# A hybrid attention and gMLP backbone: attention and its beginning rewritten as lists of steps, with a merged softmax and values in two passes

## The chip, the core and the metric

The kernel runs on one core of a Trainium2 chip. The metric is the device time of one execution in microseconds; before the change the median of three runs is 1554.76 us (1552.0 to 1555.82).

## What is computed

Two layers over 512 latent tokens of 1024 channels (a grid of 8 rows by 64 columns) with 256 context tokens, all in float32. Layer 0 mixes tokens by neighbourhood attention, layer 1 by a gated MLP over positions; each is followed by a squared-ReLU MLP. Every sub-layer begins with an RMS norm and a shift and scale that come from a conditioning vector (adaLN). The change touches layer 0's norm, its QKV products, its attention and the first part of its output projection. Of the reference, cut:

```python
q, k, v = jnp.split(h @ w_qkv, 3, axis=-1)          # 16 heads of 64
q = rms_norm(heads(q), q_g)
k = rms_norm(heads(k), k_g)
kc, vc = jnp.split(hc @ w_qkv[:, D_MODEL:], 2, axis=-1)
kc = rms_norm(heads(kc), k_g)
...
s_lat = einsum('bjqhd,bkjmhd->bhjqkm', q_r, k_r) * scale + bias
s_ctx = einsum('bjqhd,blhd->bhjql', q_r, kc) * scale
s = concatenate([s_lat, s_ctx], axis=-1)
p = softmax(s, axis=-1)
o = einsum(p_lat, v_r) + einsum(p_ctx, vc)
...
x = x + g1 * (y @ w_o)
x = x + g2 * squared_relu_mlp(modulate(rms_norm(x, norm2_g[i]), sh2, sc2), mlp_w1[i], mlp_w2[i])
```

## The kernel before

Channels lie on the 128 partitions, in eight chunks k, and tokens on the free axis. Every float32 product is made of three float32r products: both operands are parted into a high part (a cast, on ScalarE) and a low part (value less cast, on VectorE), and high by high, high by low and low by high are added up in PSUM (`products`, L178). The weights lie in one array `wall`, cut into units of 128 x 1536 (`UNIT`); class `Weights` (L48) loads a unit from HBM on SP's queue into one of two buffers `raw`, casts it in four parts into `whi` and `wlo` (L80, L81; three buffers of each), and `get` casts units ahead of their use by `ahead`.

In the beginning (L214 to L367) the instructions of TensorE, VectorE and ScalarE are pinned to program order (`in_order`, `pe_`, `vec_`, `act_`). `squares` and `root` make the norm's sum: a square, three folding additions on VectorE, one matmul with `ones`, a square root, a reciprocal. `ada_load` and `ada_rows` compute shift and scale for a group g of two chunks: 64 small matmuls, a copy of the row, its transpose, four small additions. `chunks` scales two chunks of the input and parts them into `h_hi`, `h_lo` (latent) or `hc_hi`, `hc_lo` (context); `lat_products` and `con_products` add these chunks into the QKV tiles of head pair 0, which stay open in six PSUM areas `o0`. At the end 16 matmuls spread the conditioning vector over the partitions (`cb`, L357 to L362).

Then eight pairs of heads follow (L561 to L579). `a_tile(p, t)` makes QKV of pair p for 128 tokens: latent tiles t = 0 to 3 (24 matmuls of 384 columns), context tiles 4 and 5 (24 of 256 columns, k and v alone); it squares and copies the result and parts v into `vh` and `vl`. Two heads lie in these tiles with 64 columns of zeros between, so that a window of 128 columns holds one head and zeros. After some tiles comes `ada_block` (L378), one row of the adaLN products for later use: a DMA of 512 KB and a multiplication with a sum on VectorE. `a_final(p)` normalizes q and k (a square root on ScalarE, three multiplications on VectorE, two on GpSimd), transposes them in three groups (`split`, L455) and parts them into `th` and `tl` (two buffers), from which 16 DMAs on SP's queue fill `kk`, `q1` and `q2`. `scores(n)` makes the scores of head n in four blocks of 128 queries by 512 keys (256 of a neighbourhood, 256 of the context) and the softmax: a maximum over the context half, bias and maximum over the other, two exponentials with sums, a reciprocal, a scaling on GpSimd. `values(n)` goes through six key tiles; for each, `turn` transposes the two to four blocks of probabilities that see it and parts them into `ph` and `pl` (two buffers each), and three products with `vh` and `vl` add to one PSUM bank `o` for both heads of a pair. The output projection follows (`residual`, L605): the first four output tiles are multiplied k by k, the others one by one, the last three in two halves of the tokens with the next norm between.

In the pairs the order on each engine is not pinned: a planner sorts instructions by program order and by when it takes them to be ready. PSUM has eight banks: three `mm`, two `t` (transposes), two `s` (scores and sums), one `o`.

## Time and profile before

| | us |
|---|---|
| median of three runs (1552.0 to 1555.82) | 1554.76 |
| the profiled execution | 1551.22 |
| its span | 1549.4 |
| TensorE busy | 1506.5 |
| VectorE busy | 925.4 |
| ScalarE busy | 663.8 |
| GpSimd busy | 138.1 |

Times in the rows are counted from the start of the span. A matmul's end is modelled, so a busy TensorE is not yet one at its peak: the distance from one start to the next tells more than a duration. In a row of the timeline, x4 says that four instructions in a row are put together, and the brackets name idle time before them and what ended it. The rows that the prediction uses stand further below.

### The profile page before, as it was taken

The numbers are of one execution on the slowest core, as the hardware profiler recorded it, in microseconds if no ns is written. First come the engines' busy times: TensorE is split into PE (matmuls) and PEld (weight loads), VectorE is DVE, ScalarE is ACT, GpSimd is POOL, SyncE is SP. The second block draws the span as 40 slices with busy tenths as digits, with TensorE's granted clock in tenths as the row PEclk, the third lists the DMA queues.
The fourth block names the chain that finished last, engine by engine and source line by source line (L and its number), as shares of the span: only waits on it lengthen the run. The fifth ranks groups of instructions, "written<-read, shape, count | busy, mean of one in ns | idle before, by whom it ended". The sixth has DMA issues, their size and how long they took to land.

```text
span 1549.4 us, 21490 instructions
## 1 busy us (share of the span) xinstructions
PE 1506.5 (97%) x7960; PEld 1289.4 (83%) x7960; DVE 925.4 (60%) x1953; ACT 663.8 (43%) x1569; POOL 138.1 (9%) x162
## 2 busy tenths in 40 slices
PE   4999999999999999999999999999999999999999
PEld 3888888887898888888978887888889988888888
DVE  4778777777776555665565568644456743334431
ACT  3566666675544322442443366323234532234320
POOL 0122222222200000000100013100001000000000
PEclk9999999999999999999999999999999999999999
DMA  9365555535146555556233325323221333223330
GB/s 319 137 178 172 169 165 162 168 114 165 65 143 209 199 199 191 196 192 205 90 107 136 115 93 164 118 93 115 86 95 44 140 103 100 86 100 102 102 110 28
DMA packets 69224, 212.08 MB, mean 137 GB/s; under 512 B 8320, under 2 KB 27392, under 8 KB 68736
## 3 DMA queue, kind: packets, MB, share of 16 engines
q1 hardware_dynamic: 57600, 200.57, 39.4%
q10 hardware_dynamic: 11520, 10.15, 2.2%
q8 instruction: 62, 1.02, 0.3%
q14 instruction: 42, 0.34, 0.1%
HBM read 193.91 MB, written 2.10 MB: 127 GB/s over the span
## 4 chain that ended last, share of the span: by engine, by line
PE 69%; DVE 3%; issue 0%; ACT 0%; DMA 0%; ACTq 0%; DVEq 0%
PE ps_mm L183 34%; PE ps_t L183 23%; PE ps_o L183 11%; PE ps_s L755 1%; DVE wlo L81 1%; DVE nt L172 1%; DVE hl L174 0%; DVE xall L611 0%; DMA raw<-wall 0%; PE ps_s L156 0%; DVE acc L151 0%; DVE u L761 0%; ACT v L731 0%; DVE v L733 0%; DVE hl L170 0%
## 5 line engine op out<-in xcount | busy, mean ns | idle before, releaser
L80 ACT CAST whi<-raw 128x384 fp32r<-128x384 f32 x620 | 278.4, 511 | 352.4 <-PE ps_mm L183 150.2
L81 DVE TENSOR_TENSOR wlo<-raw,whi 128x384 fp32r<-128x384 f32 x620 | 329.2, 579 | 143.3 <-ACT whi L80 142.9
L380 DVE CUSTOM_DVE_ANT_0 adaraw<-adaraw,cb 128x1024 f32<-128x1024 f32 x80 | 99.2, 1240 | 98.3 <-DMA adaraw<-ada 98.2
L183 PE MATMUL ps_mm<-hh,wlo 128*128 128x512 f32 (+1 forms) x416 | 154.0, 370 | 0.6 <-DVE wlo L81 0.6
L183 PE MATMUL ps_mm<-hh,whi 128*128 128x512 f32 (+1 forms) x416 | 154.2, 371 | 0.0
L183 PE MATMUL ps_mm<-hl,whi 128*128 128x512 f32 (+1 forms) x416 | 153.8, 370 | 0.0
L183 PE MATMUL ps_mm<-ml,whi 128*128 128x512 f32 (+1 forms) x336 | 120.7, 359 | 0.0
L183 PE MATMUL ps_mm<-mh,wlo 128*128 128x512 f32 (+1 forms) x336 | 120.5, 359 | 0.0
L183 PE MATMUL ps_mm<-mh,whi 128*128 128x512 f32 (+1 forms) x336 | 120.5, 359 | 0.0
L183 PE MATMUL ps_mm<-wlo,hh 128*128 128x384 f32 (+1 forms) x320 | 113.2, 354 | 0.7 <-DVE wlo L81 0.7
L183 PE MATMUL ps_mm<-whi,hh 128*128 128x384 f32 (+1 forms) x320 | 113.2, 355 | 0.0
L183 PE MATMUL ps_mm<-whi,hl 128*128 128x384 f32 (+1 forms) x320 | 113.0, 354 | 0.0
L183 PE MATMUL ps_t<-hh,whi 128*128 128x512 f32 (+1 forms) x280 | 104.4, 373 | 0.0
L183 PE MATMUL ps_t<-hl,whi 128*128 128x512 f32 (+1 forms) x280 | 104.1, 372 | 0.0
L183 PE MATMUL ps_t<-hh,wlo 128*128 128x512 f32 (+1 forms) x280 | 103.9, 371 | 0.0
L183 PEld LDWEIGHTS ps_mm<-hh,wlo 128*128 128x128 f32 x416 | 78.5, 189 | 13.7 <-DVE wlo L81 0.8
L183 PEld LDWEIGHTS ps_mm<-hl,whi 128*128 128x128 f32 x416 | 78.5, 189 | 12.6
L183 PEld LDWEIGHTS ps_mm<-hh,whi 128*128 128x128 f32 x416 | 78.5, 189 | 12.6
L665 ACT CAST mh<-relu 128x512 fp32r<-128x512 f32 x64 | 39.7, 622 | 95.1 <-DVE relu L662 95.1
L611 DVE SCALAR_TENSOR_TENSOR xall<-ps_mm,mod,xall 128x512 f32<-128x512 f32 (+1 forms) x47 | 30.7, 657 | 68.7 <-PE ps_mm L183 68.7
L541 ACT CAST ph<-ps_t 128x512 fp32r<-128x512 f32 (+2 forms) x96 | 45.2, 481 | 61.9 <-PE ps_t L538 56.4
L183 PEld LDWEIGHTS ps_mm<-mh,whi 128*128 128x128 f32 x336 | 63.5, 189 | 9.4
(229 smaller groups left out, 3387.9 us busy)
## 6 DMA issues: line engine op xcount, KB each, us to landing
raw<-wall SPq DMA_DIRECT2D x155, 768.0 KB, 4.4
adaraw<-ada SPq DMA_DIRECT2D x80, 512.0 KB, 3.8
aw<-ada SPq DMA_DIRECT2D x32, 256.0 KB, 7.1
bt<-bias_t SPq DMA_DIRECT2D x16, 512.0 KB, 3.8
q<-th SPq DMA_DIRECT2D x32, 128.0 KB, 2.4
q<-tl SPq DMA_DIRECT2D x32, 128.0 KB, 2.4
bc<-lngb ACTq DMA_DIRECT2D x12, 256.0 KB, 3.5
x0l<-x0T SPq DMA_DIRECT2D x2, 1024.0 KB, 9.6
```

Source lines behind the costliest of these rows:

```text
L80: nc.scalar.copy(out=hi[:, cs], in_=raw[:, cs])
L81: nc.vector.tensor_tensor(out=lo[:, cs], in0=raw[:, cs], in1=hi[:, cs], op=ALU.subtract)
L172: vec.scalar_tensor_tensor(out=t, in0=xk, scalar=A[:, k:k + 1], in1=r, op0=ALU.mult, op1=ALU.mult)
L183: eng.matmul(o, lhsT=a, rhs=b, start=start and i == 0, stop=stop and i == n - 1, skip_group_check=shared)
L380: vec.tensor_tensor_reduce(out=a, in0=a, in1=cb, scale=1.0, scalar=0.0, op0=ALU.mult, op1=ALU.add, accum_out=mod[:, idx:idx + 1])
L541: act.copy(out=ph[:, cs], in_=tb[:, cs])
L611: vec.scalar_tensor_tensor(out=x[m][:, c0:c1], in0=o[:, c0:c1], scalar=gate(m), in1=x[m][:, c0:c1], op0=ALU.mult, op1=ALU.add)
L665: act.copy(out=a, in_=r)
L755: pe.matmul(s[:, n * P:(n + 1) * P], lhsT=v[:, n, g * P:(g + 1) * P], rhs=ws, start=True, stop=True)
```

## The change

It does four things.

- In the beginning, `squares` comes in two halves; `total` adds up chunks by several matmuls in place of the folding additions (all eight chunks for the first half of the tokens, four after one addition for the others); the conditioning vector is spread first; `ada_rows` is cut into the matmuls and `ada_cols`; weights are cast part by part between other work (`casts`), and `lat_products` takes one chunk k and some of the tiles t, so that products, adaLN matmuls, sums and transposes alternate.
- The pairs become lists of steps: `a_steps` (one k of one tile), `f_steps` (norm, context keys, keys, queries), `s_steps` (one block of scores), `v_steps` (one key tile). `weave` puts the QKV steps of the next pair, or at the end the first output tiles (`o_steps`), evenly between the steps of scores and values. The probabilities of a key tile are multiplied two steps after they were turned.
- Scores of both halves get bias (zeros for the context), sign and extremum in one instruction of 512 columns and one exponential; a reciprocal is made for two blocks at a time.
- `vh` and `vl` of one head lie side by side in 128 columns of `vv`, and each key tile is multiplied by `ph` and by `pl` only. A head ends with `finish`: one half of the partitions of its bank is copied and added to the other.

The 24 rows of adaLN that are computed in the pairs are spread otherwise (`ADA`). The diff, cut to its core; the lines that it takes out are left out here, as they stand in the kernel above, and so are bodies that only move, such as the DMAs of keys and queries:

```diff
+        def squares(i):
             sq = pre.tile([P, KC, TC], F32, tag="psq", bufs=2, name="psq")
+            for ks in (slice(0, KC // 2), slice(KC // 2, KC)):
+                act_.activation(out=sq[:, ks], in_=x0[i][:, ks], func=AF.Square)
             return sq
...
+        def fold(sq):
+            h = KC // 2
+            vec_.tensor_tensor(out=sq[:, :h], in0=sq[:, :h], in1=sq[:, h:], op=ALU.add)
+        def total(sq, n):
             sps = bank("s", 2)
+            for k in range(n):
+                pe_.matmul(sps[:, :TC], lhsT=ones, rhs=sq[:, k], start=k == 0, stop=k == n - 1)
+            return sps[:, :TC]
+        def root(total, rr):
+            act_.activation(out=rr, in_=total, func=AF.Sqrt, scale=1.0 / D, bias=eps)
+            vec_.reciprocal(out=rr, in_=rr)
...
+            return row
+        def ada_cols(g, row):
             tp = bank("t", 2)
...
+            for k, t in zip(ks, ts):
                 vec_.scalar_tensor_tensor(out=t, in0=xs[:, k], scalar=A[:, k:k + 1], in1=rr, op0=ALU.mult, op1=ALU.mult)
                 act_.activation(out=hi[k], in_=t, func=AF.Identity, bias=B[:, k:k + 1])
+            for k, t in zip(ks, ts):
                 vec_.scalar_tensor_tensor(out=lo[k], in0=t, scalar=B[:, k:k + 1], in1=hi[k], op0=ALU.add, op1=ALU.subtract)
...
+        def lat_products(k, ts=range(4)):
+            for t in ts:
+                qkv_products(o0[t], t, W.get("qkv", k), k, eng=pe_)
...
+        act_.activation(out=junk, in_=eps, func=AF.Sqrt)
...
         for n in range(2):
             o = bank("s", 2)
             for i in range(4):
+                pe_.matmul(o[:, i * P:(i + 1) * P], lhsT=cc[:, 4 * n + i, 0:1].broadcast_to([P, P]), rhs=ident,
+                           start=True, stop=True)
+            act_.copy(out=cb[:, n * 512:(n + 1) * 512], in_=o)
+        sa = squares(0)
+        ta = total(sa, KC)
+        sb = squares(1)
+        fold(sb)
+        tb = total(sb, KC // 2)
+        root(ta, rl[:, :TC])
+        root(tb, rl[:, TC:])
+        row = ada_rows(0, aw[0])
+        cast = W.casts(act_, vec_)
+        cast[0]()
+        ada_cols(0, row)
+        chunks(0, lat, (), cast[1:])
+        sc = squares(2)
+        fold(sc)
+        lat_products(0)
+        row = ada_rows(1, aw[1])
+        lat_products(1, range(2))
+        ada_cols(1, row)
+        lat_products(1, range(2, 4))
+        chunks(1, lat)
+        tc_ = total(sc, KC // 2)
+        root(tc_, rc)
+        cast = W.casts(act_, vec_)
+        for step in cast:
+            step()
+        lat_products(2)
+        chunks(0, con)
+        row = ada_rows(2, aw[2])
+        lat_products(3, range(2))
+        ada_cols(2, row)
+        lat_products(3, range(2, 4))
+        chunks(1, con)
+        con_products(0)
+        chunks(2, lat)
+        con_products(1)
+        lat_products(4)
+        row = ada_rows(3, aw[3])
+        chunks(2, con)
+        lat_products(5, range(2))
+        ada_cols(3, row)
+        lat_products(5, range(2, 4))
+        con_products(2)
+        chunks(3, lat)
+        lat_products(6)
+        for step in W.casts(act_, vec_):
+            step()
+        lat_products(7)
+        chunks(3, con)
+        con_products(3)
+        for step in W.casts(act_, vec_):
+            step()
+        W.ahead = 2
...
+    NV = [3, 3, 3, 3, 3, 3]
+    vv = [[at.tile([P, 256], F32R, name=f"vv{b}_{t}") for b in range(NV[t])] for t in range(6)]
     pbuf = [at.tile([P, 640], F32, name=f"pb{i}") for i in range(NPB)]
     for b in pbuf:
+        pool.memset(b.rearrange("p (s k) -> p s k", s=2)[:, :, :64], 0.0)
+    bt = at.tile([P, 5, 256], F32, name="bt")
+    pool.memset(bt[:, 4], 0.0)
...
+    pe_ = pe
...
+        vhv, vlv = vx[:, 0:4:3], vx[:, 1:3]
...
+        if t < ADA[p]:
             with tc.issue_after(last.ins):
...
+    def a_steps(p, ts):
+        open_ = {}
+        def step(t, k):
+            if k == 0:
+                open_[t] = mm()
+            qkv_products(open_[t], t, W.get("qkv", p * KC + k), k, eng=pe_)
+            if k == KC - 1:
+                evict(p, t, open_[t])
+        return [lambda t=t, k=k: step(t, k) for t in ts for k in range(KC)]
...
+    def f_steps(p):
+        def norm():
+            st = pairs[p]
+            ss, raw = st["ss"], st["raw"]
+            act.activation(out=ss, in_=ss, func=AF.Sqrt, scale=1.0 / 64, bias=eps)
+            vec.reciprocal(out=ss, in_=ss)
+            for i, n in ((2, 4), (0, 8), (1, 8)):
+                rv = raw[i].rearrange("p t (h d) -> p (t h) d", d=64)
+                vec.tensor_tensor(out=rv, in0=rv, in1=ss[:, 8 * i:8 * i + n].unsqueeze(2).broadcast_to([P, n, 64]),
+                                  op=ALU.mult)
+            for r in (raw[0], raw[1]):
+                pool.tensor_tensor(out=r[:, :, :P], in0=r[:, :, :P],
+                                   in1=gain.rearrange("p h d -> p (h d)").unsqueeze(1).broadcast_to([P, 2, P]),
+                                   op=ALU.mult)
...
+        def keys(context):
+            if context:
...
+        def queries():
...
+        return [norm, lambda: keys(True), lambda: keys(False), queries]
...
+    def s_steps(n):
...
+            vec.tensor_tensor_reduce(out=pb, in0=s.rearrange("p (s k) -> p s k", s=2), in1=bt[:, j:5:4 - j], scale=-1.0,
+                                     scalar=3e38, op0=ALU.add, op1=ALU.min, accum_out=m[:, 0, jc])
+            last = act.activation(out=pb, in_=pb, func=AF.Exp, scale=-1.0, bias=m[:, 0, jc], accum_out=m[:, 1, jc])
+            if p >= NPAIR - 2 and j < ADA[n - 4]:
+                with tc.issue_after(last.ins):
+                    ada_block(sum(ADA[:n - 4]) + j)
+            if j % 2:
+                vec.reciprocal(out=m[:, 2, j - 1:j + 1], in_=m[:, 1, j - 1:j + 1])
+                for i in (j - 1, j):
+                    pb = pbuf[(4 * n + i) % NPB]
+                    pool.tensor_scalar(out=pb[:, 64:], in0=pb[:, 64:], scalar1=m[:, 2, i:i + 1], scalar2=0.0,
+                                       op0=ALU.mult, op1=ALU.add)
+        return [lambda j=j: step(j) for j in range(4)]
...
+    def v_steps(n):
...
         p, h = divmod(n, 2)
...
+        vs = slice(128 * h, 128 * h + 128)
+        split, o = {}, []
...
+        def multiply(i):
+            if i == 0:
+                o.append(bank("o", 1))
...
             ph, pl, cs = split[i]
...
+            for a, part in enumerate((ph, pl)):
+                pe_.matmul(o[0][:, cs], lhsT=vv[kt][p % NV[kt]][:, vs], rhs=part, start=i == 0 and a == 0,
+                           stop=i == 5 and a == 1)
...
+        def finish():
+            main, other = slice(64 * h, 64 * h + 64), slice(64 - 64 * h, 128 - 64 * h)
+            side = at.tile([P, T], F32, tag="side", bufs=1, name="side")[main]
+            act.copy(out=side, in_=o[0][other])
             if p < NPAIR - 1:
+                vec.tensor_tensor(out=rowmajor(OT[p][main]), in0=grid(o[0][main]), in1=grid(side), op=ALU.add)
             else:
+                vec.tensor_tensor(out=side, in0=o[0][main], in1=side, op=ALU.add)
+                act.copy(out=rowmajor(oh[p][main]), in_=grid(side))
+                vec.tensor_tensor(out=rowmajor(ol[p][main]), in0=grid(side), in1=rowmajor(oh[p][main]), op=ALU.subtract)
...
+        def step(i):
+            if i > 1:
+                multiply(i - 2)
+            if i < 6:
+                turn(i)
+            if i == 7:
+                finish()
+        return [lambda i=i: step(i) for i in range(8)]
+    def weave(main, fill):
+        for i, e in enumerate(main):
+            e()
+            for f in fill[i * len(fill) // len(main):(i + 1) * len(fill) // len(main)]:
+                f()
+    def o_halves(k):
+        act.copy(out=oh[k], in_=OT[k])
+        vec.tensor_tensor(out=ol[k], in0=OT[k], in1=oh[k], op=ALU.subtract)
+    o_open = {}
...
+    def o_steps(ms, ks):
+        def step(m, k):
+            if k == 0:
+                o_open[m] = mm() if m < 3 else bank("s", 2)
+            products(o_open[m], [(W.get("o", m * NPAIR + k), (oh[k], ol[k]))], k == 0, k == NPAIR - 1, eng=pe_)
+        return [lambda m=m, k=k: step(m, k) for k in ks for m in ms]
     for t in range(6):
+        evict(0, t, o0[t])
+    f = f_steps(0)
+    f[0]()
+    a = a_steps(1, (0, 1, 4))
+    weave([lambda: None, f[1], f[2], f[3]], a[:12] + a[12:])
     for p in range(NPAIR):
+        s = s_steps(2 * p)
+        v = v_steps(2 * p - 1) if p else []
         if p + 1 < NPAIR:
+            fill = a_steps(p + 1, (5, 2, 3))
+        else:
+            fill = o_steps(range(3), range(2, 5))
+        weave(v[:2] + s[:2] + v[2:3] + s[2:] + v[3:], fill)
+        s = s_steps(2 * p + 1)
+        v = v_steps(2 * p)
+        if p + 1 < NPAIR:
+            f = f_steps(p + 1)
+            if p + 2 < NPAIR:
+                fill = a_steps(p + 2, (0, 1, 4))
+            else:
+                for k in range(6):
+                    o_halves(k)
+                fill = o_steps(range(3), range(2))
+            weave(f[:1] + s[:2] + v[:1] + s[2:] + v[1:2] + f[1:2] + v[2:3] + f[2:3] + v[3:4] + f[3:] + v[4:], fill)
+        else:
+            o_halves(6)
+            weave(s[:2] + v[:1] + s[2:] + v[1:], o_steps(range(3), range(5, 7)))
+    W.ahead = 1
+    weave(v_steps(2 * NPAIR - 1), o_steps((3,), range(7)))
+    for f in o_steps(range(4), (7,)):
+        f()
+    W.ahead = 2
...
+        for m in opened:
+            update(m, opened[m], 0, T, pool)
+        for m in range(len(opened), KC - tail):
             o = mm()
```

## Rows read from the trace of the kernel before

**Rows 1.** The page's first part: busy time of each engine and share of the span.
```profile
PE 1506.5 (97%) x7960; PEld 1289.4 (83%) x7960; DVE 925.4 (60%) x1953; ACT 663.8 (43%) x1569; POOL 138.1 (9%) x162
```
**Rows 2.** Table of stretches: length, busy us of each engine, granted clock, DMA.
```profile
14.60:70.80 56.20, 45.14 (x426) 38.73 (x427) 38.03 (x76) 24.31 (x50) 7.08 (x36) 0.91 0.72 250
70.80:386.50 315.70, 306.54 (x1855) 273.06 (x1854) 245.64 (x753) 205.92 (x617) 71.31 (x80) 1.00 0.53 159
...
430.00:1549.40 1119.40, 1113.17 (x5397) 938.94 (x5395) 605.35 (x1062) 405.68 (x851) 50.25 (x32) 1.00 0.38 126
```
**Rows 3.** Timeline of TensorE in the beginning: start, us, instruction, idle time before.
```profile
14.61 1.19 PE L243 MATMUL ps_s<-psq,ones 128*128 128x256 f32 x2 [14.61 <-DVE psq L243]
...
25.63 0.44 PE L243 MATMUL ps_mm<-whi,hh 128*128 128x384 f32 x1 [2.16 <-ACT hh L243]
...
32.02 1.95 PE L243 MATMUL ps_s<-aw,cc 128*32 128x128 f32 x64
...
37.16 0.69 PE L243 MATMUL ps_mm<-whi,hh 128*128 128x384 f32 x1 [2.47 <-ACT hh L243]
...
43.77 0.67 PE L243 MATMUL ps_s<-psq,ones 128*128 128x256 f32 x2 [0.57 <-DVE psq L243]
...
70.83 0.39 PE L183 MATMUL ps_mm<-whi,hh 128*128 128x384 f32 x1
```
**Rows 4.** Table of stretches around three spells of the clock (seventh number).
```profile
25.60:30.00 4.40, 4.20 (x14) 3.88 (x15) 2.17 (x3) 0.72 (x1) 0.00 (x0) 0.63 1.00 400
...
37.10:40.30 3.20, 3.14 (x9) 2.79 (x10) 2.74 (x5) 1.66 (x3) 0.00 (x0) 0.50 1.09 346
...
49.20:54.00 4.80, 4.61 (x16) 4.29 (x17) 4.80 (x10) 2.83 (x6) 0.00 (x0) 0.65 0.00 2
```
**Rows 5.** Timeline of TensorE in attention.
```profile
78.51 0.85 PE L459 MATMUL ps_t<-ident,raw 128*128 128x128 f32 x6 [0.36 <-DVE raw L445]
...
186.85 0.33 PE L183 MATMUL ps_mm<-whi,hh 128*128 128x384 f32 x1
187.02 0.34 PE L183 MATMUL ps_mm<-wlo,hh 128*128 128x384 f32 x1
188.19 0.63 PE L459 MATMUL ps_t<-ident,raw 128*128 128x128 f32 x4 [0.83 <-DVE tl L463]
...
385.03 0.44 PE L183 MATMUL ps_o<-pl,vh 128*128 128x384 f32 x1
```
**Rows 6.** Groups of VectorE until 70.8 us: form, count, busy us, mean ns, idle before.
```profile
L81 DVE TENSOR_TENSOR wlo<-raw,whi 128x384 fp32r<-128x384 f32 x16 | 8.2, 552 | 0.5 <-ACT whi L80 0.5
...
L243 DVE SCALAR_TENSOR_TENSOR hl<-h,mod,hh 128x512 fp32r<-128x512 f32 x8 | 6.0, 751 | 4.3 <-ACT hh L243 4.3
...
L243 DVE SCALAR_TENSOR_TENSOR hcl<-h,modc,hch 128x256 fp32r<-128x256 f32 x8 | 3.9, 483 | 3.5 <-ACT hch L243 3.5
```
**Rows 7.** Timeline of ScalarE, the cast of the first weights.
```profile
20.98 1.75 ACT L80 CAST whi<-raw 128x384 fp32r<-128x384 f32 x4 [1.70 <-DMA raw<-wall]
```
**Rows 8.** Groups of TensorE, forms kept apart: a value pass of 384 columns.
```profile
L183 PE MATMUL ps_o<-pl,vh 128*128 128x384 f32 x32 | 11.0, 342 | 0.4 <-DVE pl L542 0.2
```
**Rows 9.** The chain that ended last, in order of time: one piece of layer 0's MLP.
```profile
541.64 21.76 PE ps_t L183 x96
```
**Rows 10.** Groups of VectorE and ScalarE between 120 and 360 us.
```profile
L542 DVE TENSOR_TENSOR pl<-ps_t,ph 128x384 fp32r<-128x384 f32 (+2 forms) x77 | 42.1, 557 | 23.9 <-ACT ph L541 22.8
...
L380 DVE CUSTOM_DVE_ANT_0 adaraw<-adaraw,cb 128x1024 f32<-128x1024 f32 x19 | 23.2, 1222 | 7.3 <-DMA adaraw<-ada 7.3
L504 DVE CUSTOM_DVE_ANT_0 pb<-ps_s,bt,sm 128x256 f32<-128x256 f32 x48 | 22.4, 478 | 0.1
L503 DVE TENSOR_REDUCE sm<-ps_s 128x1 f32<-128x256 f32 x50 | 20.4, 418 | 2.9 <-PE ps_s L501 2.6
...
L541 ACT CAST ph<-ps_t 128x384 fp32r<-128x384 f32 (+2 forms) x76 | 36.0, 483 | 48.7 <-PE ps_t L538 43.2 <-DVE pl L542 3.3 <-DVE sm L503 1.8
```
**Rows 11.** Waits of TensorE between 70.8 and 386.5 us: total, times, longest.
```profile
PE ps_o L183 <- ACT ph L541: 1.8, 3, 0.8
```

269 lines of the change are left out of this document (74 added, 195 removed).

## The prediction

> **What bounds the kernel now.** The page's first part says that TensorE holds 97% of the span [rows 1], so I read next where the missing time and the avoidable matmuls lie. The table of stretches [rows 2] parts the span into the beginning (to 70.8 us), attention with the first part of its output projection (70.8 to 386.5) and the rest from 430 us, where TensorE is busy 1113.17 of 1119.40 us. Nothing in the diff reaches that last stretch except the order in which it takes its PSUM banks, so some 1120 us stay as they are, and the 43.5 us between carry the same products. What can move is the first 386.5 us: 56.2 us of the beginning hold 45.14 us of busy TensorE, and the 315.7 us of attention hold 306.54. In attention TensorE is the bound nearly everywhere, VectorE is busy 245.64 us and ScalarE 205.92 in the same stretch. So attention gains what its matmuls lose, and a little idle time; the beginning is a chain of waits.
>
> **The beginning.** Its order on each engine is written out by hand, and the timeline of TensorE [rows 3] shows what this costs: the first sums of squares at 14.61, the first QKV product at 25.63, a block of 64 adaLN matmuls (1.95 us) at 32.02, the transpose of their row, then 2.47 us of nothing until the next product at 37.16, waiting for the chain of addition, scaling and ScalarE's cast. The table of stretches shows the granted clock just behind this gap at 0.50 [rows 4]: TensorE had idled, and the products ran at 1.2 instead of 2.4 GHz. Nine of them took 3.14 us that take 9 x 0.17 = 1.6 at the full clock. There are three such spells, behind three such gaps; their 39 products and the like took 11.95 us instead of some 6.7, which is 1.7 or so each.
>
> From 25.63 to 70.83 are 45.2 us. The work in them: 96 latent products of 384 columns at 0.17 us from start to start [rows 5], 16.6 (with 0.173 before rounding); 48 context products of 256 columns at about 0.12 (an estimate by columns from 0.17 for 384 and 0.227 for 512), 5.8; three adaLN blocks 5.9; the sum of squares of the context 0.7; 16 matmuls for the copy of the conditioning vector, some 1.8; transposes 0.6. That is 31.4, so 13.8 us are slack. The change spreads the latent products over single chunks k, puts half of a chunk between a row's matmuls and its transpose, and gives each engine its next piece before the old chain ends; both spells after the first should go with the gaps that precede them. What is late next is VectorE. It still has in this stretch 16 subtractions for the weight casts (8.2 us), 16 instructions of 512 columns for the latent chunks (6.0 for the half shown, and as much for the other), 16 of 256 columns (3.9, twice) [rows 6], and some 5 for the adaLN columns, a reciprocal and a fold: 33 us, next to TensorE's 32. So I leave 4.2 us of slack, one cold spell and 2.5 us of waits for VectorE: 9.6 gained.
>
> The first product itself moves little. The first weights are cast at 20.98, at the end of a wait for their DMA [rows 7], and the change moves none of the loads ahead of it. Row transpose, columns, one scaled chunk and its cast follow, 3.4 us by the same steps as before, which gives 24.4 at best. The new sums of squares take 8 and 4 matmuls instead of one each; one of them (two passes) took between 0.67 and 1.19 us [rows 3], so 5.4 to 9.5 and 2.7 to 4.8 us, most of it before the first weights are there; at the long end the adaLN block behind them, and the first product, come 3 us later than before. I take 25.0, a gain of 0.6, bounds +1.2 and -3. The context's sum costs 4 x 0.67 less the old 0.7, 2.0 more; the 16 conditioning matmuls go to an idle TensorE at 5 us, 1.8 less. The additions that are dropped from VectorE's tree, and the early load of the Sqrt table, lie beside DMA waits and count nothing. Sum: 9.6 + 0.6 - 2.0 + 1.8 = 10, bounds 5 and 14.
>
> **Values in two passes.** For each head and key tile the old kernel multiplies ph and pl by vh, and ph by vl. Now vh and vl of one head stand side by side in 128 columns of weights, and two passes (ph, pl) give both halves of the partitions; the product pl by vl is extra and free. One pass in three goes: 32 of 384 columns [rows 8], 32 of 512 and 32 of 256. By their starts a 512-column pass takes 21.76 us / 96 = 0.227 us where nothing waits [rows 9], the others 0.173 and 0.12: 32 x 0.52 = 16.6 us, all on TensorE's path. The weight load of 128 columns stays one for each pass and hidden as before. A rule of the Trainium skill would make less of this: the page "TensorE: Matmul & The Clock Gate", section "Back-to-back issue gap", gives about 131 ns for a sustained 512-column matmul and 81 ns for 128 columns; interpolated (my estimate from that page) 96 passes would be worth 11 us. The trace does not agree, with 227 ns over 96 in a row.
>
> The price: each head now ends with a copy of one half of the bank (ScalarE) and an addition (VectorE), instead of one copy for each pair. The bank for the output has one buffer, so the next head's first multiplication, and all transposes and fill queued behind it on TensorE, wait for about 0.6 + 0.7 us. Elsewhere two turns, two or more score steps and their fill lie between; only between heads 14 and 15 are there no more than two turns (0.7 us) and one or two fills of 0.68.
>
> **Merged softmax.** Per score block one 512-column instruction with a minimum replaces a maximum (418 ns), a 256-column one (478 ns) and three small ones [rows 10]. Its price is not in the trace; by the 256-column row and the 1024-column form of the same instruction (1222 ns for the adaLN sums) [rows 10] it lies near 0.73 us, between 0.48 and 0.96. VectorE saves some 2 us for each head after paying the new addition, ScalarE about 1.5 (one exponential and one accumulator read instead of two). Neither engine is the bound, so this is worth nothing by itself; it shortens the queues that TensorE's waits come out of.
>
> **Order and waits of attention.** Printed idle of TensorE there is 315.7 - 306.5 = 9.2 us [rows 2]. A gap costs more than it prints: the one at 187.02 shows 0.83 and costs 188.19 - 187.02 - 0.17 = 1.00 [rows 5]. Counted in this way there are 21 of 0.25 us and more, the first before 78.51, the last before 385.03 [rows 5], 13 us together; 11 of them stand before the q and k transposes of a pair, because these wait for VectorE's norm or for th/tl buffers that DMAs still read. In the new lists norm, context keys, keys and queries are four steps with scores and values between them, and no value is multiplied until two steps after its turn. The cast and the subtraction between take 0.48 + 0.56 us [rows 10]; two steps are at least 1.7 us of TensorE. So I expect 8 of the 13 us back, bounds 0 and 14 (the upper one adds small waits). The adaLN sums are only redistributed: 24 as before, six on pair 1 and three on later ones, 1.2 us of VectorE each, and their loads and the 16 q/k copies of a pair stay on SP's queue; the last four list steps of a head and two turns, 5 us and more, lie between the queries' copies and the first score that needs them.
>
> **The end of attention** loses cover: the first seven k of four output tiles are now fill inside the last heads, and when head 15 is done only its own chain (copy, addition, cast, 0.6 each) stands between TensorE and the eighth. The scheduler can pull tile 4 forward. I take 1.5 us lost, with heads 14 and 15 above, bounds 0 and 4.
>
> **Sum.** 10 + 16.6 + 8 - 1.5 = 33.1 us. The profiled execution took 1551.2, so 1518; it is 3.5 under the median of the three runs, 1554.8, and the forecast for that median is 1521. Bounds: 1554.8 less 5 + 16.6 + 0 - 4 gives 1537, less 14 + 16.6 + 14 gives 1510.
>
> **Rivals.**
> The lists do not set the order. In attention the instructions are not pinned, and the planner may sort them by its own idea of readiness as it did before; then the waits stay and only passes and beginning count: 1554.8 - 16.6 - 10 + 1.5 = 1530. For it: the old timeline already has other products among its turns and q/k transposes amid QKV products [rows 5]. Against it: with norm, keys and queries apart, even a free sorting has more to put in front of a wait. 15%.
> The beginning gains nothing, as VectorE's 33 us or a longer cold spell before the first product take the place of the gaps: 1531. 10%.
> Turning becomes the bound. A head has six turns, with two buffers each for ph, pl and their bank; TensorE's next turn waits for VectorE's subtraction two turns before. If VectorE, in order behind an adaLN sum (1.2 us) or a norm, is late by x at each of 96 turns, the price is 96x. At 0.2 us each the time is 1521 + 19 = 1540; from 0.34 us on it is slower than before, and at 0.5 us 1569. Against it: TensorE's waits for ph in the old kernel come to 1.8 us in all of attention [rows 11]. 8%, of which slower 5%.
> Passes cheaper than columns, as the page's rule has it: 16.6 becomes 11, so 1527. 1%; the 227 ns speak against it.
> All waits go and the beginning closes: under 1510, 5%.
>
> **Chances.** Forecast 61%. The range 1510 to 1537 holds the forecast, the first two rivals and the fourth, and leaves out 13%. What a measurement tells from no change is 0.3%, 4.7 us: faster 0.92, within 0.03, slower 0.05.
>
> **What would show it.** In the changed profile: 64 instead of 96 value passes of each width; first QKV product near 25 us and the last of pair 0 near 61; no clock of 0.50 after some 30 us; few waits before the q/k transposes; attention over near 352 us. It is wrong if TensorE's waits name ph or pl, if the 512-column minimum is far over 0.96 us, or if VectorE's share in attention rises over 90%.

## The result and the profile after

The changed kernel takes 1534.18 us (median of four runs, 1530.83 to 1536.67) against 1555.29 for the kernel before: ratio 0.9866, 95% interval 0.9842 to 0.9891, so 21 us less. The forecast was 1521 and its range ended at 1537. The direction held; of 34 us forecast, 13 did not come. The profiled execution took 1535.0 us, its span is 1533.1.

The first part of the page after, to be read against [rows 1]: TensorE's busy time fell by 15.5 us only, VectorE's by 24.3.

```profile
PE 1491.0 (97%) x7890; PEld 1280.4 (84%) x7890; DVE 901.1 (59%) x1739; ACT 653.8 (43%) x1455; POOL 135.6 (9%) x135
```

Tables of stretches (length, busy us of each engine, granted clock, DMA) show where it went. First the kernel after: beginning, first score to last value pass, and layer 0's MLP, taken from TensorE's first sum for the norm ahead of it to the first sum for the next norm.

```profile
14.60:61.59 46.99, 39.45 (x421) 34.40 (x421) 35.27 (x72) 21.39 (x49) 1.54 (x9) 0.93 0.79 277
...
79.50:362.80 283.30, 271.92 (x1659) 247.32 (x1659) 214.23 (x515) 185.54 (x463) 71.34 (x78) 1.00 0.54 167
383.40:744.90 361.50, 353.38 (x1709) 297.77 (x1709) 220.69 (x405) 123.45 (x268) 12.71 (x11) 0.99 0.52 173
```

The same two stages of the kernel before:

```profile
88.10:387.10 299.00, 290.30 (x1759) 257.31 (x1759) 233.74 (x724) 197.52 (x586) 69.42 (x78) 1.00 0.53 161
411.10:761.50 350.40, 349.45 (x1708) 296.44 (x1709) 221.46 (x405) 123.57 (x268) 12.78 (x11) 1.00 0.52 177
```

The beginning ends 9.2 us earlier (61.59 against 70.83), attention is 15.7 us shorter, and the MLP, in which the change touches nothing but the order of banks, is 11.1 us longer with the same instructions in the same order on TensorE, VectorE and ScalarE. The stretch between attention and the MLP is 3.4 us shorter (20.6 against 24.0), so the two profiled spans differ by 16.3 us; the medians differ by 21, as the profiled execution of before lay 4 us under its median. TensorE's waits name the engine to look at (total, times, longest); first attention, then the MLP:

```profile
PE ps_o L619 <- DVE pl L610: 6.3, 6, 1.7
...
PE ps_o L202 <- ACT mh L777: 6.4, 2, 3.7
```

The lists put the multiplication of pl two steps behind its turn, and still TensorE stands there six times. Around one of these stops the timelines of SP's queue, VectorE and TensorE show why (start, us, instruction, idle time before):

```profile
217.46 0.34 SPq L428 DMA_DIRECT2D adaraw<-ada  x1
...
222.04 1.22 DVE L429 CUSTOM_DVE_ANT_0 adaraw<-adaraw,cb 128x1024 f32<-128x1024 f32 x1 [1.29 <-DMA adaraw<-ada]
223.19 0.08 DVE L429 DVE_READ_ACCUMULATOR2_ANT mod<- 128x1 f32 x1
223.19 0.42 DVE L610 TENSOR_TENSOR pl<-ps_t,ph 128x256 fp32r<-128x256 f32 x1
...
222.27 0.28 PE L202 MATMUL ps_mm<-whi,hcl 128*128 128x256 f32 x1
223.66 0.39 PE L619 MATMUL ps_o<-pl,vv 128*128 128x256 f32 x1 [1.11 <-DVE pl L610]
```

A row of adaLN was read at 217.46 and its sum began at 222.04, when it had landed; VectorE stood for it from 220.75, then summed it for 1.2 us, and the subtraction for pl, whose ph had been cast at 221.18, came behind it at 223.19: VectorE took nothing ahead of the waiting sum. The MLP shows the same with another victim:

```profile
668.35 0.79 PE L202 MATMUL ps_o<-mh,whi 128*128 128x512 f32 x1 [2.70 <-ACT mh L777]
...
671.48 1.23 DVE L429 CUSTOM_DVE_ANT_0 adaraw<-adaraw,cb 128x1024 f32<-128x1024 f32 x1 [0.59 <-DMA adaraw<-ada]
...
672.63 0.69 DVE L774 SCALAR_TENSOR_TENSOR relu<-ps_t,relu 128x512 f32<-128x512 f32 x1
...
673.35 0.62 ACT L777 CAST mh<-relu 128x512 fp32r<-128x512 f32 x1 [2.91 <-DVE relu L774]
...
674.02 0.80 PE L202 MATMUL ps_o<-mh,whi 128*128 128x512 f32 x1 [3.73 <-ACT mh L777]
```

A hidden tile's relu is queued behind a row, and ScalarE's mh waits for the relu. When the second product of the MLP needs the last tiles, they are late. In the whole stage VectorE stood for rows 49 times, 102.4 us (52 times, 90.9 us, in the kernel before); and with the stops of TensorE the granted clock is 0.50, which is 1.2 GHz, for ten microseconds. The first line is of the kernel before, the others of the kernel after:

```profile
DVE adaraw L380 <- DMA adaraw<-ada: 90.9, 52, 4.6
```

```profile
DVE adaraw L429 <- DMA adaraw<-ada: 102.4, 49, 5.0
...
668.00:678.20 10.20, 6.13 (x12) 3.85 (x13) 5.77 (x10) 4.71 (x11) 0.00 (x0) 0.50 0.63 212
```

Rows set their own pace. They have one tile, so the next read goes out when the sum before it is done: the sum that began at 661.02 ended at 662.24, and the next read was issued at 662.28. The chain that ended last, followed back from the last instruction, runs through such reads in the MLP after, up to the late product (start, us):

```profile
656.18 4.81 DMA adaraw<-ada
667.07 4.39 DMA adaraw<-ada
675.97 33.74 PE ps_mm L202 x144
```

The kernel before had the same rows and the same order there, and stood 1.0 us from this. Its last mh was cast at 691.49, over at 692.11, and TensorE took it at 693.12 (the ml of that tile was over at 692.83 and taken at 693.35):

```profile
691.49 0.62 ACT L665 CAST mh<-relu 128x512 fp32r<-128x512 f32 x1 [3.14 <-DVE relu L662]
...
692.14 0.69 DVE L666 TENSOR_TENSOR ml<-relu,mh 128x512 fp32r<-128x512 f32 x1 [0.69 <-ACT mh L665]
...
693.12 0.39 PE L183 MATMUL ps_mm<-mh,whi 128*128 128x512 f32 x1
693.35 0.39 PE L183 MATMUL ps_mm<-ml,whi 128*128 128x512 f32 x1
```

So the theory to test, A: rows that land late hold VectorE, and the change bared that. Rivals: B, an accident of one execution; C, the new start of the banks; D, the traffic of the rows rather than the waiting.

### The profile page after: what moved, and what is told of

Its sections match the earlier page's. It is cut to its first block, busy times and chain, and to the rows that moved or that the text cites. A ratio compares the mean times of both kernels' runs of the same rounds, so it can differ in the third digit from the quotient of the medians.

```text
span 1533.1 us, 20932 instructions
## 1 busy us (share of the span) xinstructions
PE 1491.0 (97%) x7890; PEld 1280.4 (84%) x7890; DVE 901.1 (59%) x1739; ACT 653.8 (43%) x1455; POOL 135.6 (9%) x135
## 4 chain that ended last, share of the span: by engine, by line
PE 72%; DMA 14%; DVE 8%; issue 2%; ACT 2%; SPq 1%; POOL 0%; ACTq 0%; DVEq 0%; POOLq 0%
PE ps_mm L202 36%; PE ps_t L202 19%; DMA adaraw<-ada 12%; PE ps_o L202 10%; DVE adaraw L429 2%; PE ps_o L619 1%; DVE wlo L83 1%; PE ps_s L867 1%; DMA aw<-ada 1%; PE ps_t L606 1%; PE ps_s L566 1%; DMA raw<-wall 1%; PE ps_s L567 1%; DVE nt L179 1%; DVE pl L610 1%
## 5 line engine op out<-in xcount | busy, mean ns | idle before, releaser
L82 ACT CAST whi<-raw 128x384 fp32r<-128x384 f32 x604 | 271.2, 511 | 348.7 <-PE ps_mm L202 158.1
L83 DVE TENSOR_TENSOR wlo<-raw,whi 128x384 fp32r<-128x384 f32 x604 | 321.6, 582 | 143.0 <-ACT whi L82 142.6
L202 PE MATMUL ps_mm<-hh,whi 128*128 128x512 f32 (+1 forms) x400 | 149.5, 375 | 0.0
L202 PE MATMUL ps_mm<-hh,wlo 128*128 128x512 f32 (+1 forms) x400 | 149.2, 373 | 0.3 <-DVE wlo L83 0.3
L202 PE MATMUL ps_mm<-hl,whi 128*128 128x512 f32 (+1 forms) x400 | 149.2, 373 | 0.0
L202 PE MATMUL ps_mm<-whi,hh 128*128 128x384 f32 (+1 forms) x320 | 116.4, 364 | 1.3 <-DVE vv L472 1.3
L202 PE MATMUL ps_t<-hh,wlo 128*128 128x512 f32 (+1 forms) x312 | 112.8, 362 | 0.6 <-DVE wlo L83 0.6
L202 PE MATMUL ps_t<-hh,whi 128*128 128x512 f32 (+1 forms) x312 | 113.4, 364 | 0.0
L202 PE MATMUL ps_t<-hl,whi 128*128 128x512 f32 (+1 forms) x312 | 113.4, 363 | 0.0
L579 POOL TENSOR_SCALAR pb<-pb,sm 128x576 f32<-128x576 f32 x64 | 58.4, 925 | 154.8 <-DVE sm L576 112.9
```

Source lines behind the costliest of these rows:

```text
L82: act.copy(out=hi[:, cs], in_=raw[:, cs])
L83: vec.tensor_tensor(out=lo[:, cs], in0=raw[:, cs], in1=hi[:, cs], op=ALU.subtract)
L202: eng.matmul(o, lhsT=a, rhs=b, start=start and i == 0, stop=stop and i == n - 1, skip_group_check=shared)
L579: pool.tensor_scalar(out=pb[:, 64:], in0=pb[:, 64:], scalar1=m[:, 2, i:i + 1], scalar2=0.0, op0=ALU.mult, op1=ALU.add)
```

## The experiments

Stages by the traces, in us, and the ratio to the kernel before in the same comparison. "Scores" is the time of TensorE's first score product; "attention" runs from there to the last value pass; "MLP" is layer 0's, as above. What follows it takes 787.9 to 788.8 in all. Each row of stages is one profiled execution; attention differs by 2.3 us between e1 and e2, whose code and order of TensorE's instructions are the same up to its end.

| kernel | scores | attention | MLP | ratio (95%) |
|---|---|---|---|---|
| before | 88.1 | 299.0 | 350.4 | 1 |
| after, first profile | 79.5 | 283.3 | 361.5 | 0.9866 (0.9842 to 0.9891) |
| e1 after again | 80.0 | 282.5 | 358.8 | 0.9876 (0.9861 to 0.9891) |
| e2 banks from 0 | 80.3 | 284.8 | 355.8 | 0.9880 (0.9866 to 0.9895) |
| e3 short rows | 77.6 | 274.1 | 350.7 | 0.9737 (0.9721 to 0.9754) |
| e4 second tile in the MLP | 79.0 | 282.9 | 356.4 | 0.9845 (0.9829 to 0.9861) |
| e5 rows a slot late | 79.2 | 283.0 | 350.4 | 0.9783 (0.9764 to 0.9803) |
| e6 before, short rows | 88.1 | 299.6 | 350.4 | 0.9982 (0.9971 to 0.9992) |
| e7 third pass | 78.2 | 292.1 | 352.1 | 0.9854 (0.9834 to 0.9875) |
| e8 softmax apart | 79.9 | 293.3 | 358.9 | 0.9892 (0.9866 to 0.9917) |
| e9 rows at 0, 2, 3 | 78.5 | 280.4 | 351.1 | 0.9806 (0.9790 to 0.9823) |
| e10 beginning alone | 78.7 | 299.4 | 350.4 | 0.9944 (0.9930 to 0.9959) |
| e11 short rows, third pass | 77.8 | 286.7 | 350.4 | 0.9837 (0.9820 to 0.9853) |
| e12 attention alone | 91.1 | 284.4 | 358.1 | 0.9952 (0.9935 to 0.9969) |

**e1, the changed kernel again.** No edit.

> The changed kernel once more, unaltered. In its first trace TensorE stands 6.4 us for mh at 665 to 674 us, in layer 0's MLP, and its clock then falls to half for 10 us; the rows of ada land there 4.2 us after their issue (3.8 in the trace of the kernel before), and VectorE finishes one row in 5.5 us (5.25 before). Theory A (the rows hold VectorE, and the change only altered how late they come): the stall is there again, in the same place, whenever the rows need 5.5 us; time 1531 to 1537. Rival B (one execution's accident: rows land in 3.8 us here, the stall is gone, and some 10 us with it): 1522 to 1526.

1533.53 us, the stop for mh is there (3.9 us at once), the MLP takes 358.8. B falls, though the size of the stop varies (6.4 us in the first profile).

**e2, the banks.**

```diff
-    banks = [3]
+    banks = [0]
```

> The changed kernel with the rotation of PSUM banks behind attention begun at bank 0 as before, not at 3; nothing else. Rival C (another bank holds the tile that TensorE waits on in the MLP): the 6.4 us for mh and the half clock behind it go, 1522 to 1526. Theory A (rows): the waits for mh stay within 2 us of 6.4, 1531 to 1537.

1534.52 us. The waits for mh are 2.7 us, less than expected of A (within 2 us of 6.4) and not gone as expected of C; the MLP is 3.0 us shorter than in e1. But the first sum for the norm behind attention comes 4.6 us later than in e1, and no time is gained. Part of that is this execution's own: the code and TensorE's order up to there are those of e1, and here the granted clock fell to 0.50 for 3.4 us, which it did not in e1's attention:

```profile
349.30:352.70 3.40, 3.40 (x10) 2.69 (x9) 2.58 (x7) 2.60 (x7) 0.30 (x1) 0.50 1.02 428
```

C falls as the cause: the stop is there with either start of the banks.

**e3, short rows.**

```diff
+    row_tile = cbp.tile([P, D], F32, name="adaraw")
+    pool.memset(row_tile, 0.0)
...
-        a = cbp.tile([P, D], F32, tag="adaraw", name="adaraw")
-        nc.sync.dma_start(out=a, in_=ada1[i])
+        a = row_tile
+        nc.sync.dma_start(out=a[:, :P], in_=ada1[i][:, :P])
```

> The changed kernel with each row of ada read in 128 of its 1024 columns (64 KB, not 512 KB) into a tile that keeps its place; VectorE's sum runs over all 1024 as before, over zeros and stale numbers in the rest, so most of layer 0's later and layer 1's modulation is left out. VectorE's work is unchanged, only the landing is shorter. Theory A: no wait of TensorE for mh, no clock at half at 668, the gaps of 0.7 to 1.8 us ahead of the value products of pl (seven of them, 6.9 us) go to under 2 us: 1534 - 10 - 5 = 1516 to 1521. Rivals B and C: no change beyond 2 us.

1512.53 us, better than A asked for. TensorE's waits ahead of products of pl fall from 6.3 to 0.2 us in attention, VectorE's idle time ahead of rows there from 11.5 to 1.0 us, and the MLP has no stop for mh or ml:

```profile
DVE adaraw L432 <- DMA adaraw<-ada: 1.0, 2, 0.6
...
77.60:351.70 274.10, 271.42 (x1666) 248.00 (x1665) 214.63 (x513) 185.97 (x464) 70.88 (x78) 1.00 0.46 135
372.40:723.10 350.70, 349.48 (x1709) 296.38 (x1709) 221.34 (x405) 126.46 (x268) 12.32 (x11) 1.00 0.32 106
```

Rows in full cost the changed kernel about 21 us: 8 in attention, 8 in the MLP, 2 ahead of the scores, the rest within what the executions differ by. Whether the wait or the traffic costs this, e3 cannot tell, as it takes away both; and with shorter reads the planner also sorted part of the instructions otherwise (TensorE's in attention, VectorE's in both stages).

**e4, a second tile in the MLP.**

```diff
-        a = cbp.tile([P, D], F32, tag="adaraw", name="adaraw")
+        where = second[0] if i % 2 else cbp
+        a = where.tile([P, D], F32, tag="adaraw", name="adaraw")
...
+            second[0] = sp
```

> The changed kernel with a second tile for ada's rows in layer 0's MLP alone (rows of odd number go to it), so that a row is read while the one before it is summed; the attention keeps the single tile. Theory A: the idle time of VectorE ahead of rows falls from some 38 us to under 10 in the MLP, no wait for mh, no half clock there: 1522 to 1526; attention ends at 363 us as now. If the rows' DMA rate is itself the limit (a row each 4.2 us against 5.44 us of products), still enough. Rivals B and C: within 2 us of the unaltered kernel.

1529.77 us, a smaller gain than expected. VectorE's idle time ahead of rows in the MLP fell from 102.4 to 23.1 us, not to under 10 (the 38 of the expectation are the part of the stage from 600 us on). The stop of the second half went and another came in the first: a row idles VectorE for 1.43 us, and an ml that was ready waits behind it. Reading rows earlier did not help at this place, where a sum still stood in the queue ahead of what TensorE needed.

```profile
493.03 1.22 DVE L432 CUSTOM_DVE_ANT_0 adaraw<-adaraw,cb 128x1024 f32<-128x1024 f32 x1 [1.43 <-DMA adaraw<-ada]
...
494.93 0.63 PE L202 MATMUL ps_o<-ml,whi 128*128 128x512 f32 x1 [3.52 <-DVE ml L782]
```

**e5, rows a slot late.**

```diff
+    def slot(last, n, limit):
+        with tc.issue_after(last.ins):
+            while waiting:
+                row_sum()
+            for _ in range(n):
+                if loaded[0] < limit:
+                    row_load(loaded[0])
+                    loaded[0] += 1
...
+            if second[0] is not cbp:
+                slot(last, 2, 80)
...
-                    for _ in range(2):
-                        if nxt < ada_to:
-                            with tc.issue_after(last.ins):
-                                ada_block(nxt)
-                            nxt += 1
+                    slot(last, 1, ada_to)
```

> The changed kernel with the sum of each ada row queued one place later than its read: where a row was read and summed, the row read at the place before is summed and the next one read. In layer 0's MLP there is one row per hidden tile and two per residual tile, with a second tile for rows of odd number there; all 80 rows are read and summed in full. Theory A (VectorE stands ahead of a row that has not landed, and TensorE behind it): the seven gaps ahead of the pl products in attention go to under 2 us and the wait for mh goes, as with short rows (1512.5 us): 1512 to 1518. Rival D (it was not the waiting but the 512 KB that each row moves, which slow the q, k and weight transfers): no better than the kernel with two tiles in the MLP, 1526 to 1531.

1523.16 us with all rows in full, between the two ranges. The MLP is back at 350.4; neither TensorE nor VectorE has a wait that a row ended there, while the stage moved as much as before (177 GB/s in both). So the waiting cost this stage its 11 us, as A says, and not the traffic as such. Three things changed at once, though: one row for a hidden tile in place of two, a second tile, and the sum a slot later. Of these only the second tile was tried alone (e4, 356.4). The stage in the table of stretches:

```profile
382.90:733.30 350.40, 349.45 (x1709) 296.36 (x1709) 222.41 (x405) 125.77 (x268) 12.16 (x11) 1.00 0.53 177
```

Attention is not shorter. TensorE no longer waits for pl ahead of products of values, but ahead of q and k transposes (1.8 us) and turns (1.2), and VectorE still idles 6.7 us ahead of rows (1.7 at 296.73): that row's read went out at 291.56, on SP's queue between the copies for kk and those for q. The copies for q behind it land in 4.2 us, 2.4 in the kernel before (56 of the 64 for th and tl have a row in flight beside them); those for kk, 4.5 in the kernel after, are back at 2.4. And from 345.60 on the granted clock was 0.50 for 3.4 us, behind turns that waited for GpSimd's scaling, so not all of the 8.9 us over short rows is the rows'.

```profile
DVE adaraw L435 <- DMA adaraw<-ada: 6.7, 10, 1.7
...
345.60:349.00 3.40, 3.40 (x9) 2.48 (x10) 2.96 (x7) 1.72 (x5) 0.00 (x0) 0.50 1.02 430
...
q<-th SPq DMA_DIRECT2D x32, 128.0 KB, 4.2
...
kk<-th SPq DMA_DIRECT2D x16, 128.0 KB, 2.4
...
291.56 0.61 SPq L429 DMA_DIRECT2D adaraw<-ada  x1
...
292.27 0.46 SPq L551 DMA_DIRECT2D q<-th  x1
```

**e6, short rows in the kernel before.** The edit of e3.

> The kernel before with each row of ada read in 128 of its 1024 columns; the sums run as before, so most of the modulation is left out. It asks how much the rows cost before the change, where VectorE stood 98 us ahead of them in all but TensorE had no wait longer than 0.25 us in layer 0's MLP. Theory E (before the change the rows were covered and the change bared them): within 5 us of 1553, so 1548 to 1553. Theory F (they cost TensorE as much before, in the gaps ahead of the q and k transposes, which the prediction booked as the order of the work): 1532 to 1543.

1553.66 against 1556.67 us, 0.2%: E holds, F falls. (In layer 0's MLP before, one wait of TensorE is 0.6 us, for a wlo; the others are shorter than 0.25 or at the norm's sums.) Before the change short rows give back 3 us, after it 21: the rows were covered before, and after the change they are not.

**e7, a third pass.**

```diff
-            for a, part in enumerate((ph, pl)):
+            for a, part in enumerate((ph, pl, pl)):
...
-                           stop=i == 5 and a == 1)
+                           stop=i == 5 and a == 2)
```

> The changed kernel with a third pass of values, that of pl repeated, so that the output counts it twice: 96 matmuls more, 32 each of 512, 384 and 256 columns. By the prediction's price (0.227, 0.173, 0.120 us) +16.6 us: 1550. If the passes fill time in which TensorE waits for rows anyhow (6.9 us of gaps ahead of the products of pl): +9 to +13, 1543 to 1547.

1533.91 us: 96 more matmuls cost no time that can be told. Attention is 9.6 us longer than in e1 and the MLP 6.7 shorter: its instructions stand in the same order as in e1, but rows landed sooner (3.6 us at the median in this stage, 4.0 in e1), and TensorE waits for mh 0.8 us only. Why they did is open. Both expectations missed on the time, by what happened outside attention; the 9.6 there agree with the second.

**e11, short rows and the third pass.** The edits of e3 and e7.

> The changed kernel with short rows (128 of 1024 columns read, the modulation mostly left out) and the third pass of values, that of pl counted twice. With short rows alone: 1512.5 us. By the prediction's price of the passes, with no row to wait for: +16.6, 1529. In the kernel with full rows the same 96 matmuls moved attention's end by 7.6 us alone; if they cost that by themselves and not because the rows' waits took them in: 1520.

1526.83 us; 0.9837 against 0.9737 for e3: 1.0%, 15.5 us, of which 12.6 lie in attention by the two profiles (274.10 us in e3):

```profile
77.80:364.50 286.70, 285.57 (x1762) 262.31 (x1761) 215.19 (x513) 187.26 (x464) 70.77 (x78) 1.00 0.44 129
```

So with short rows the passes cost between three quarters and nearly all of what the prediction gave for them, nearer to 1529 than to 1520.

**e8, the softmax apart.**

```diff
-            vec.tensor_tensor_reduce(out=pb, in0=s.rearrange("p (s k) -> p s k", s=2), in1=bt[:, j:5:4 - j], scale=-1.0,
-                                     scalar=3e38, op0=ALU.add, op1=ALU.min, accum_out=m[:, 0, jc])
-            last = act.activation(out=pb, in_=pb, func=AF.Exp, scale=-1.0, bias=m[:, 0, jc], accum_out=m[:, 1, jc])
+            vec.reduce_max(m[:, 0, jc], s[:, 256:], axis=AX.X)
...
+            last = act.activation(out=pb[:, 0], in_=pb[:, 0], func=AF.Exp, bias=m[:, 1, jc], accum_out=m[:, 3, jc])
```

> The changed kernel with the softmax as before: per block a maximum of 256 columns, the sum with the bias and its maximum on 256, a sign, two exponentials of 256, a sum and a reciprocal, in place of one pass of 512 on VectorE, one exponential and a shared reciprocal. By the rows of before VectorE then has some 0.8 us more per block (1.55 against 0.77 and half a reciprocal), 51 us over 64 blocks, at 75% busy now: to 92%. If VectorE has room: under +3 us, 1533 to 1537. If VectorE is what the row waits push over the edge: +8 to +20 us, 1541 to 1554.

0.9892 against 0.9876 for e1, intervals overlapping; but in its profile attention is 10.8 us longer than in e1, with VectorE at 81% (236.19 of 293.30 us) and new waits of TensorE (that profile is the slowest of e8's four executions, 1543.54 against 1537.9 to 1541.49):

```profile
PE ps_t L607 <- POOL pb L580: 5.9, 6, 1.6
PE ps_t L607 <- DVE tl L515: 3.6, 3, 2.6
```

One of these waits, 2.6 us, goes back to a buffer tl that a copy for kk still read, and the granted clock was 0.50 for 3.4 us behind it. So the softmax apart costs something up to 11 us; neither expectation is met clearly, and VectorE got to 81%, not the 92 expected.

**e9, other tiles for the rows.** The edit against e5.

```diff
-    ADA = (0, 6, 3, 3, 3, 3, 3, 3, 0, 0, 0, 0)
+    ROWS_AT = [()] + [range(6)] + [(0, 2, 3)] * 6
...
-        if t < ADA[p] or waiting:
-            slot(last, t < ADA[p], 24)
+        if t in ROWS_AT[p]:
+            with tc.issue_after(last.ins):
+                row_load(loaded[0])
+                row_sum()
+            loaded[0] += 1
```

> The kernel of the run before with rows a slot late, whose MLP is kept as it was there; in attention, from pair 2 on, the three rows go to the tiles 0, 2 and 3 in place of 0, 1 and 2, each read and summed at its own tile. A row is then read among no q and k transfers of its half (tile 1's was issued at 217.46 us between two of them and landed 4.6 us later, ahead of the pl product that TensorE waited for). If the row at tile 1 is what bares the gaps: attention's end 5 to 8 us earlier, 1515 to 1518. If any row read late in its own tile does it: no change, 1521 to 1525.

1522.47 us, no better than e5 by the ratios, as the second theory has it. VectorE's waits for rows did fall to 1.8 us, and attention to 280.4, 6.3 above short rows; it ends 3.3 us earlier than in e5, not 5 to 8. Little of what is left is a wait for a row: TensorE's stops name pl ahead of turns (2.0), of q and k transposes (1.4) and of products (0.7), GpSimd's scaling (1.6), a vv (1.3). The copies for q are back at 2.4 us to landing, but the larger ones for kk, 2.4 in e5, take 3.5:

```profile
q<-th SPq DMA_DIRECT2D x32, 128.0 KB, 2.4
...
kk<-th SPq DMA_DIRECT2D x16, 128.0 KB, 3.5
```

In e9 it is not rows that hold up these copies: of all 64 for kk, 46 have a load of the bias (512 KB too) in flight beside them and land in 3.7 us, 9 have neither bias nor row and land in 2.4. So D is not ruled out in attention, where a row slows the copies beside it in the kernel after and in e5; but taking the rows away from them, as here, brought the bias there and hardly any time. Whether such traffic or the order of instructions makes the 6 us was not told apart.

**e10 and e12, the parts alone.** All up to the last product of pair 0 from the one kernel, all behind it from the other.

> The kernel before with the new beginning alone (all up to the last product of pair 0), attention and the rest as before. By the prediction's term 10 us go (bounds 5 to 14); the trace of the changed kernel has pair 0 done 9.2 us earlier: 1556 - 9 = 1545 to 1548. If what follows gives it back (attention or the MLP waiting for something with a clock of its own, such as transfers): 1552 to 1556.

> The beginning of the kernel before, with all behind it (attention as lists, merged softmax, two value passes, the banks' start) as in the changed kernel. If the parts add up: the changed kernel's 21 us less the beginning's 8, so 13 us below the kernel before, ratio 0.990 to 0.994, with the wait of TensorE for mh in layer 0's MLP as there. If that wait is an accident of one order of instructions and goes here: 21 us below, ratio 0.985 to 0.988. By the prediction's terms for attention (16.6 + 8 - 1.5): 23 us below, 0.985.

The beginning alone gives 0.9944, 8.7 us (6.4 to 10.9), as expected. Attention alone gives 0.9952, 7.5 us (4.8 to 10.1), with the stop for mh as in the changed kernel (4.9 us) and the MLP at 358.1. Together 16, against 19 to 21 for both: they add up within the intervals. Attention alone gave less than each of its three expectations (13, 21 and 23 us); the interval reaches the lower end of the first, 10.

## Why the prediction came out where it did

The time lies inside the range and the direction was right, but the range holds it partly by luck: it gave nothing for the stretch that lost 11.1 us, and its upper end was made of other terms (a poorer beginning, no waits gained, a dearer end of attention).

**The sentence that failed** is the one ahead of all sums: nothing in the diff reaches the last stretch, so 1120 us stay as they are [rows 2]. The instructions and their order stay; the margin didn't. The profile of before showed TensorE at 349.45 of 350.40 us in the MLP, and I took a full engine for a safe one. One microsecond separated mh from its product. From the first sum of a row in the MLP to the 47th, which stands ahead of the last mh, it was 243.8 us before and 253.3 after, that is 5.30 and 5.51 for each row: 9.5 more, with 1.0 in hand, leave 8.5 us by which that product came late (stops of 6.8 and products at half clock between them); half clock behind it makes most of the rest of the 11.1.

Eight kernels have this stage in the same order on TensorE, VectorE and ScalarE, with rows in full. They differ in how long the rows take, and the stops go with that (one profile each):

| kernel | first to 47th sum, us | TensorE's waits for mh and ml, us | MLP, us |
|---|---|---|---|
| e10 | 242.4 | 0 | 350.4 |
| before | 243.8 | 0 | 350.4 |
| e7 | 245.7 | 1.0 | 352.1 |
| e2 | 247.6 | 2.9 | 355.8 |
| e1 | 249.6 | 4.1 | 358.8 |
| e12 | 250.6 | 5.1 | 358.1 |
| e8 | 250.8 | 5.3 | 358.9 |
| after | 253.3 | 6.8 | 361.5 |

By the margin of before, stops should begin where the rows take more than 243.8 + 1.0 = 244.8 us, and they do. Why the rows take longer is open (last section).

**Beginning, 10 us, bounds 5 and 14:** 9.2 by the trace, 8.7 by e10. Right, and in the main for its reason: the first product is at 23.96 (25.0 forecast), pair 0 ends at 61.59 (61), and one spell of half clock (6.8 us) is left of three. The stretch between took 37.6 us, 36 forecast, and the earlier first product made up for it. The pieces, on TensorE's timeline:

```profile
23.96 0.69 PE L193 MATMUL ps_mm<-whi,hh 128*128 128x384 f32 x1 [3.12 <-ACT hh L193]
...
61.59 0.45 PE L202 MATMUL ps_mm<-whi,hh 128*128 128x384 f32 x1 [1.29 <-DVE vv L472]
```

**Values, 16.6 us:** the count is right (64 passes of each width), and the price nearly so with short rows (12.6 to 15.5 in e11). What is doubtful is "all on TensorE's path". In the kernel with full rows the third pass put back costs attention 9.6 us (e7), 3 less than with short rows, and TensorE's waits for pl ahead of products fall with it from 6.3 to 3.6: some of the passes taken away were also time in which a row could land. The 3 us rest on single profiles. The group of 256-column passes of pl, with its idle time:

```profile
L619 PE MATMUL ps_o<-pl,vv 128*128 128x256 f32 x32 | 10.3, 321 | 6.1 <-DVE pl L610 6.1
```

**Waits of attention, 8 us, bounds 0 and 14:** the old ones did go; no stop before q and k transposes names the norm or tl. Each distance from one start to the next, less the median for its width (0.231, 0.174, 0.120 and 0.108 us for 512, 384, 256 and 128 columns over the three traces), adds up to 23.6 us lost by TensorE in attention before, 21.9 after and 11.6 with short rows. So 12 were there to be had, and 2 came; other waits took the places, the six ahead of products of pl (6.3 us) above all. Forecast for attention's end was 352; it is 362.8 after and 351.7 in e3. The step at fault reads "the adaLN sums are only redistributed ... 1.2 us of VectorE each". I counted the sums' busy time and left out the 7.3 us that VectorE stood ahead of them [rows 10], with what is queued behind such a wait; in attention after it stood 11.5 us.

**End, 1.5 us lost:** none. From the last value pass to the norm's first sum it is 20.6 us against 24.0, and 16 more projection products (3.6 us) lie ahead of that pass.

**Merged softmax, nothing by itself:** the 512-column minimum takes 0.69 us (0.73 estimated), and VectorE is at 76% in attention, with 19.5 us less work there:

```profile
L569 DVE CUSTOM_DVE_ANT_1 pb<-ps_s,bt 128x512 f32<-128x512 f32 x48 | 32.2, 686 | 4.2 <-issue 1.9 <-PE ps_s L567 1.9 <-DMA bt<-bias_t 0.2
```

That it is worth nothing is neither borne out nor refuted in its size (e8).

**Rivals.** The third came nearest: TensorE waits for pl, as its sign said, behind an adaLN sum, as its condition said. But it comes at six places of 96, at 1 us each, not at each turn; and it is the row in full, not its sum, that sets the price, as e3 kept the sums. Two of the prediction's own signs came against it: TensorE's waits name pl, and the clock was at 0.50 once more after 30 us, in the MLP.

A kernel that takes the change and spreads the rows, with each sum one slot after its read (e5), needs 1523.16 us, 0.9783 of the kernel before. It beats both. Attention is 9 us longer there than with short rows, 6 in e9, and was not won.

## What to carry to other kernels

In these traces an instruction that waited for a DMA on VectorE was a stop for all that was queued behind it; read and use in different slots, with fewer reads in a row and a second tile, gave layer 0's MLP back its time, though not attention. A part of the kernel that runs at full rate still has a margin: before a change that alters timing ahead of it, find in the trace the operand that arrives last and how long before its use it does. And ask of a removed instruction not only what time it took but also what it covered.

## What the runs showed of the hardware

The same reads of 512 KB landed later in kernels with the new attention, also in the MLP, far from it; the page's list of DMA issues, before and after (KB each, median us to landing):

```profile
adaraw<-ada SPq DMA_DIRECT2D x80, 512.0 KB, 3.8
```

```profile
adaraw<-ada SPq DMA_DIRECT2D x80, 512.0 KB, 4.2
```

By these medians it is 3.8 in the kernel before and 3.6 in e10, 4.2 in after and e8, 4.0 in e1, e2 and e7, 3.9 in e12. In the MLP alone it is 3.5 and 3.4 against 3.8 to 4.0, and 3.6 in e7. The cause stayed open.

A row of 64 KB landed in 2.1 us, half the time of one of 512 KB. In the kernel after, the 54 copies for q with a row of 512 KB in flight beside them landed in 3.9 us at the median, the 10 without one in 2.4.

The granted clock was 0.50, that is 1.2 GHz, for some 3.4 us behind one stop of 3.5 us (e4, from 491.4). In e5 it was so for 3.4 us from 345.60 on, behind no stop longer than 0.6 us; ahead of it turns of 128 columns had come in twos, with short waits between, and TensorE had been busy for 2.69 of 4.00 us:

```profile
343.01 0.44 PE L617 MATMUL ps_t<-ident,pb 128*128 128x128 f32 x2 [0.17 <-POOL pb L590]
343.74 0.44 PE L617 MATMUL ps_t<-ident,pb 128*128 128x128 f32 x2 [0.29 <-POOL pb L590]
344.46 0.44 PE L617 MATMUL ps_t<-ident,pb 128*128 128x128 f32 x2 [0.29 <-POOL pb L590]
345.47 0.70 PE L630 MATMUL ps_o<-ph,vv 128*128 128x512 f32 x1 [0.57 <-ACT ph L620]
```
